# Hybrid decoder trunk on one core: the mixer's tables, taps and first output units in another order, and three smaller rearrangements

## The chip, the core and the metric

The kernel runs on one core of one Trainium2 chip. The metric is the device time of one execution in microseconds (us), the median of several runs. A core has TensorE (PE in the rows; PEld is its weight load), VectorE (DVE), ScalarE (ACT), GpSimd (POOL) and SyncE (SP), which here only issues transfers.

## The reference, cut to what matters

One sequence of 256 tokens with 16 learned positions in front (272 positions, width 1024) goes through two layers and a last RMSNorm, all in float32.

```python
for layer in range(2):
    if layer == 0:
        h = h + even_mixer(rms_norm(h, g), ...)     # recurrent block (RG-LRU) and a state space model (S5), side by side
        h = h + swiglu(rms_norm(h, g), w_gate, w_up, w_down)          # dense, 3072 wide
    else:
        h = h + gla_mixer(rms_norm(h, g), ...)                        # chunked gated linear attention
        h = h + moe_swiglu(rms_norm(h, g), router_w, ...)             # top 2 of 8 experts, each 3584 wide
return rms_norm(h, final_norm)[:, 16:]

def even_mixer(h, ...):
    z = h @ w_in                                    # 1024 gate columns, 1024 recurrent columns, 512 S5 columns
    rec = rg_lru(causal_conv(recurrent), ...)       # a = exp(-8 r softplus(-lam)); b = sqrt(1 - a^2) * i * x; h = a h + b
    a_out = gelu(gate) * rec
    b_out = s5_ssm(s5_columns, ...)                 # complex diagonal states, 32 groups of 16 channels, then a GLU
    return concatenate([a_out, b_out]) @ w_out
```

## The kernel before

Positions lie along the free dimension (272 columns), channels on the 128 partitions, eight chunks of 128 channels. Stages follow each other: mixer (to about 178 us), dense SwiGLU (to about 400), attention (to about 555), experts (to about 1549), last norm.

**Weights.** All weights come as tiles of 1 MB (class `Stream`, DMA line L115 on SyncE's queue, tile number = place in the file). Two units of 1024 columns make a tile. Some matrices are used as float32 as they are (`fraw`, L245). For the others (`fs`, `out_part`, lines L224 to L226) a unit is first split into two parts: `split` lets ScalarE copy the high part (`whi`, L144) and VectorE subtract it for the low part (`wlo`, L146), and each product takes three matmuls. `st.unit(u)` splits unit u and the two behind it. Until the attention stage the tiles lie in a ring of R1 = 3 buffers (`ring1`), so a load can start when a buffer's last reader is through. The mixer's input units are tiles 0 to 11 (two column blocks of S5 input, then `rec`, `gates` and `zgate` blocks in the order of MIX_ORDER: tile 9 holds zgate 2 and 3, tile 10 zgate 4 and 5, tile 11 zgate 6 and 7), tile 12 the GLU, tile 13 and on the output projection, whose first unit is `B_OUT // 8`.

**Order.** PE, ACT, DVE and POOL run their instructions in the order in which the code is written (`manual_schedule`). `step(o, evac, n)` runs what is due, lets `evac` be run one step later, and runs n entries of the list `fill`. In the mixer `fill` holds the S5 tables (`tables`, L527 to L529, twelve pieces that grow from 16 to 512 columns, all on DVE) and the S5 state pieces. The SP queue is sorted by the framework.

**Mixer around the change.** `rec(m)` makes one block of the recurrent branch; its evacuation is one ACT instruction (L575) and three of DVE (L578) into `xc`. `gates(b)` multiplies blocks 2b and 2b+1 of `xc`. `s5_tp` and `s5_x` (L591, L602) prepare the S5 input. `zgate(m)` makes one block of the gate branch, evacuated by ACT (L562). There are four PSUM buffers for these blocks (tag "mm"). `lru_exp` is 16 ACT instructions (L690, L691), `lru_sqrt` four (L695), `lru_scan(b)` four of DVE (L698 to L701). `s5_direct(cc)` (L654) makes the S5 taps of one quarter in PSUM (`kp`); `s5_taps` copies them (ACT L659, POOL L660) and `s5_shift` places them with ten transfers into `KT` (L668). `out_taps(3)` is some 9 us of POOL. Then `s5_local` (L798, reads KT), `s5_out` (L810), `mix_lru` (DVE L839, then high part `mh` on ACT L829 and low part `ml` on POOL L831), and the output projection `out_part` (tiles wo).

```python
        zgate(2, 3)
        s5_x(7)
        fill.extend(s5_states(1))
        for b in range(4):
            lru_exp(b)
        s5_direct(0)
        zgate(3, 2)
```

**Dense stage.** `resid_add` adds the mixer's output, and `split_chunk` writes the eight chunks of `xg` (ACT L258, DVE L259), one by one. Group m = 0 of the dense stage needs all eight in turn, first for gate, then for up. `norm_mm` (L280) sums the squares; its result is first needed by the evacuation of gate 0.

**Start and end.** At the start SP issues the first four loads of `hT` and the two halves of tile 0. At the end the last expert's second half (`yps`) is split into `Y` high and low (L1496, L1497), `combine` multiplies both by a one-hot matrix (L1501, L1502) and adds into X (L1504), then `squares`, `gains` (L1562) and `finish` (L1565 on, output DMA L1571).

Of the kernel before, what the change touches and what calls it, by code (L numbers as in the profile page):

```python
# [8 lines left out]
F32 = mybir.dt.float32  # L9
# [7 lines left out]
P = 128  # L17
# [151 lines left out]
def trunk(ctx: ExitStack, tc: tile.TileContext, xt, pv, pw, cst, gfin, wf, wm, out, dbg=None):  # L169
# [25 lines left out]
    pwt = resid.tile([P, NPW - 1024], F32, name="pwt")  # L195
    nc.sync.dma_start(pvt, pv)
    st.load_to(0)
    nc.sync.dma_start(hT[:, 0:2], xsrc[:, 0:2])
    nc.sync.dma_start(st.raw[0][:, :UW], wf[0, :, :UW])
    for a in range(2, ND, 2):  # L200
        nc.sync.dma_start(hT[:, a:a + 2], xsrc[:, a:a + 2])
    nc.sync.dma_start(st.raw[0][:, UW:], wf[0, :, UW:])
# [109 lines left out]
    with ExitStack() as mx:  # L312
# [255 lines left out]
        def rec(m, n=0):  # L568
            b, j = divmod(m, 2)
            if j == 0:  # L570
                xc[b] = slot(f"xc{b}")
            x_ = xc[b][:, j]

            def evac(o):
                act.activation(x_, o, AF.Identity, scale=cw[:, 3, m:m + 1], bias=pvs("conv_b")[:, m:m + 1])  # L575
                for k in range(3):
                    d = 3 - k
                    dve.scalar_tensor_tensor(x_[:, d:], o[:, :NT - d], cw[:, k, m:m + 1], x_[:, d:], op0=ALU.mult,  # L578
                                             op1=ALU.add)

            step(fraw(B_REC[m], 8, raw_x(xn), NT), evac, n)
# [136 lines left out]
        shuffle()  # L718
        rec(1, 1)
        rec(2, 1)  # L720
        rec(3, 3)
        halves(C0[0][:, :, None], lambda o, sl: act.activation(o[:, :, 0], cre[sl], AF.Copy))
        halves(C0[1][:, :, None], lambda o, sl: act.activation(o[:, :, 0], cim[sl], AF.Copy, scale=-1.0))
        powers()
        gates(0)
        bg(2)
        rec(4, 2)
        s5_tp(0)
        rec(5, 2)
# [29 lines left out]
        out_taps(1)  # L759
        gated(3)  # L760
        out_taps(2)
        zgate(2, 3)
        s5_x(7)
        fill.extend(s5_states(1))
        for b in range(4):
            lru_exp(b)
        s5_direct(0)
        zgate(3, 2)
        for b in range(4):
            lru_sqrt(b)  # L770
        s5_direct(1)
        lru_scan(0)
        zgate(4, 2)
        s5_direct(2)
        lru_scan(1)
        zgate(5, 2)
        s5_direct(3)
        s5_taps()
        s5_shift()
        out_taps(3)  # L780
        lru_scan(2)
        zgate(6, 20)
# [62 lines left out]
        s5_local(1)  # L845
        s5_out(0)
        low = mix_lru(2, low)
        st.unit(B_OUT // 8)
        s5_out(1)
        low = mix_lru(3, low)  # L850
        low()
# [50 lines left out]
    with ExitStack() as fx:  # L902
        fp = phase(fx, "fp")
        fw = phase(fx, "fw", 4)
        ph = fp.tile([P, NFF, NT], F32R, name="ph")
        pl = fp.tile([P, NFF, NT], F32R, name="pl")
        zgs = {}

        def gate_evac(m, o):
            zg = zgs[m] = fw.tile([P, NT], F32, name="zg")  # L910
            dve.tensor_tensor(zg, o, rstd, op=ALU.mult)
            if m:
                after(1, lambda: act.activation(zg, zg, AF.Silu))
            else:
                act.activation(zg, zg, AF.Silu)

        def up_evac(m, o):
            zg = zgs.pop(m)
            zu = fw.tile([P, NT], F32, name="zu")
            dve.tensor_tensor(zu, o, rstd, op=ALU.mult)  # L920
            dve.tensor_tensor(zu, zu, zg, op=ALU.mult)
            after(1, lambda: act.activation(ph[:, m], zu, AF.Copy))
            after(2, lambda: dve.tensor_tensor(pl[:, m], zu, ph[:, m].bitcast(F32), op=ALU.subtract))

        for m in range(NFF):
            lag = 3 if m == 0 else 1
            if m == 1:
                norm_mm()
            step(fs(B_F + 16 * m, 8, xs_norm(), NT), lambda o, m=m: gate_evac(m, o), lag=lag)
            step(fs(B_F + 16 * m + 8, 8, xs_norm(), NT), lambda o, m=m: up_evac(m, o), lag=lag)  # L930
# [567 lines left out]

    def combine(e, d, i):
        o = psum("x", "cmb")  # L1500
        pe.matmul(o, OHT[e][:, i], Ys[e, d][0], start=True, stop=False)  # L1501
        pe.matmul(o, OHT[e][:, i], Ys[e, d][1], start=False, stop=True)  # L1502
        a = X[:, i, 512 * d:512 * d + 512]
        dve.scalar_tensor_tensor(a, o, gat[:, i, e:e + 1], a, op0=ALU.mult, op1=ALU.add)  # L1504

    hcur = None
    for s in range(E * NF + 1):
# [42 lines left out]
    fs4 = ep.tile([P, 2, 2], F32, name="fs4")  # L1550
    fs2 = ep.tile([P, 2], F32, name="fs2")

    def part(t, i, d):
        return t[:, i, 512 * d:512 * d + 512]

    def squares(d):
        for i in range(2):
            act.activation(sqs[:, i], part(X, i, d), AF.Square, accum_out=fs4[:, i, d:d + 1])

    def gains(d):  # L1560
        for i, eng in enumerate((dve, pool)):
            eng.tensor_tensor(part(ys, i, d), part(X, i, d), gft[:, 512 * d:512 * d + 512], op=ALU.mult)  # L1562

    def finish():
        dve.tensor_tensor(fs2, fs4[:, :, 0], fs4[:, :, 1], op=ALU.add)  # L1565
        inv_root(fs2, fs2, D)
        for d in range(2):
            act.activation(part(ys, 1, d), part(ys, 1, d), AF.Copy, scale=fs2[:, 1:2])
            dve.tensor_scalar(part(ys, 0, d), part(ys, 0, d), fs2[:, 0:1], None, op0=ALU.mult)
            for i in range(2):  # L1570
                nc.sync.dma_start(out[P * i:P * i + P, 512 * d:512 * d + 512], part(ys, i, d))  # L1571

    sqs = ew.tile([P, 4, 512], F32, name="sqs", tag="xq0", bufs=1)
    ys = ew.tile([P, 2, D], F32, name="ys", tag="xq1", bufs=1)
# [11 lines left out]
    with tc.If(cnt > CAP):  # L1586
# [200 lines left out]
```

## Time and profile before

| what | value |
|---|---|
| runs shown | 1566.23, 1572.45, 1572.51 us; median 1572.45 |
| profiled execution, its own time | 1565.07 us |
| its span | 1563.0 us |
| TensorE busy | 1521.8 us (97%) |
| VectorE busy | 1297.5 us (83%) |
| ScalarE busy | 1055.9 us (68%) |

The time of the profiled execution is 2.1 us above its span. Times in the rows count from the start of the span. A busy TensorE is no TensorE at its peak: matmuls overlap and their ends are modelled, so what is read is where its instructions start and what the idle time before one waited for.

### The profile page before, as it was taken

The page shows a single profiled execution, that of the slowest core. Times are in us where ns is not written, and L with a number is a line of the kernel's source. Part 1 is how long each engine was busy: PE and PEld are TensorE (multiplying, and loading weights), DVE is VectorE, ACT ScalarE, POOL GpSimd, SP SyncE. Part 2 cuts the span into 40 slices and gives each one's busy share as a digit, 9 for nine tenths or more (in the row PEclk, how much of TensorE's full clock was granted, in tenths as well). Part 3 has the DMA queues.
Part 4 walks back from the last instruction along what each step waited for, and adds up shares of the span by engine and source line. Part 5 has one row for each costly group of instructions (what it writes and reads, how often), then busy time and mean ns, then how long its engine had stood idle before and what let it go on. Part 6 is the DMA issues. An engine that isn't in the chain of part 4 may idle for free.

```text
span 1563.0 us, 21942 instructions
## 1 busy us (share of the span) xinstructions
PE 1521.8 (97%) x8306; PEld 1317.7 (84%) x8306; DVE 1297.5 (83%) x1464; ACT 1055.9 (68%) x1297; POOL 165.4 (11%) x260
## 2 busy tenths in 40 slices
PE   8998999999989989999999999999999999999996
PEld 7788999999889977888888888888888888888885
DVE  5687676655595669999999999999999999999996
ACT  3345544444543578887887787887887887777875
POOL 8952100001251200000000000000000000000000
PEclk9999999999999999999999999999999999999998
DMA  7333455454336758999899999999999999999960
GB/s 249 116 119 117 165 183 186 163 184 168 111 105 243 275 204 311 366 376 354 335 365 356 373 366 352 347 365 352 365 367 365 362 351 353 360 365 373 356 240 30
DMA packets 68897, 433.56 MB, mean 277 GB/s; under 512 B 14384, under 2 KB 14768, under 8 KB 17072
## 3 DMA queue, kind: packets, MB, share of 16 engines
q1 hardware_dynamic: 68784, 432.09, 74.2%
q8 instruction: 67, 1.10, 0.3%
q14 instruction: 46, 0.38, 0.1%
HBM read 429.80 MB, written 1.05 MB: 276 GB/s over the span
## 4 chain that ended last, share of the span: by engine, by line
PE 82%; DVE 4%; issue 3%; ACT 2%; POOL 0%; DVEq 0%; ACTq 0%; POOLq 0%
PE gu L1455 13%; PE gu L1457 13%; PE gu L1456 13%; PE yp L1484 7%; PE yp L1486 7%; PE yp L1485 7%; PE acc L225 5%; PE acc L224 5%; PE acc L226 5%; PE etp L1465 2%; DVE wlo L146 1%; ACT whi L144 1%; PE cmb L1502 0%; PE cmb L1501 0%; PE go L225 0%
## 5 line engine op out<-in xcount | busy, mean ns | idle before, releaser
L146 DVE TENSOR_TENSOR wlo<-raw,whi 128x1024 fp32r<-128x1024 f32 x788 | 959.3, 1236 | 130.7 <-ACT whi L144 99.1
L144 ACT ACTIVATE whi<-raw 128x1024 fp32r<-128x1024 f32 x788 | 825.0, 1060 | 261.6 <-PE acc L225 99.3
L1455 PE MATMUL gu<-whi,xq 128*128 128x512 f32 x896 | 357.7, 399 | 0.7 <-ACT whi L144 0.7
L1456 PE MATMUL gu<-wlo,xq 128*128 128x512 f32 x896 | 350.3, 391 | 2.4 <-DVE wlo L146 2.4
L1457 PE MATMUL gu<-whi,xq 128*128 128x512 f32 x896 | 351.5, 392 | 0.0
L1456 PEld LDWEIGHTS gu<-wlo,xq 128*128 128x128 f32 x896 | 168.5, 188 | 38.4 <-DVE wlo L146 4.2
L1457 PEld LDWEIGHTS gu<-whi,xq 128*128 128x128 f32 x896 | 168.3, 188 | 37.9
L1455 PEld LDWEIGHTS gu<-whi,xq 128*128 128x128 f32 x896 | 168.5, 188 | 34.8 <-ACT whi L144 1.5
L1484 PE MATMUL yp<-whi,hh 128*128 128x512 f32 x448 | 176.0, 393 | 0.0
L1486 PE MATMUL yp<-whi,hlw 128*128 128x512 f32 x448 | 175.7, 392 | 0.0
L1485 PE MATMUL yp<-wlo,hh 128*128 128x512 f32 x448 | 174.9, 390 | 0.0
L224 PE MATMUL acc<-xg,whi 128*128 128x272 f32 (+1 forms) x576 | 169.6, 294 | 1.7 <-DVE slab L1116 0.9
L226 PE MATMUL acc<-xg,wlo 128*128 128x272 f32 (+1 forms) x576 | 167.3, 290 | 1.9 <-DVE wlo L146 1.9
L225 PE MATMUL acc<-xg,whi 128*128 128x272 f32 (+1 forms) x576 | 166.9, 290 | 0.8 <-DVE xg L259 0.5
L224 PEld LDWEIGHTS acc<-xg,whi 128*128 128x128 f32 x576 | 110.1, 191 | 3.4 <-DVE slab L1116 1.3
L226 PEld LDWEIGHTS acc<-xg,wlo 128*128 128x128 f32 x576 | 109.8, 191 | 2.2 <-DVE wlo L146 2.2
L225 PEld LDWEIGHTS acc<-xg,whi 128*128 128x128 f32 x576 | 110.1, 191 | 1.5 <-DVE xg L259 1.4
L1562 POOL TENSOR_TENSOR ys<-X,gft 128x512 f32<-128x512 f32 x2 | 2.9, 1456 | 996.0 <-DVE X L1504 996.0
L1486 PEld LDWEIGHTS yp<-whi,hlw 128*128 128x128 f32 x448 | 84.2, 188 | 18.9
L1485 PEld LDWEIGHTS yp<-wlo,hh 128*128 128x128 f32 x448 | 84.2, 188 | 18.7 <-DVE wlo L146 0.3
L1484 PEld LDWEIGHTS yp<-whi,hh 128*128 128x128 f32 x448 | 84.2, 188 | 17.5
L245 PE MATMUL acc<-xfn,raw 128*128 128x272 f32 x320 | 77.6, 400 | 5.7 <-DMA raw<-in_wf_dram 5.7
(522 smaller groups left out, 1753.5 us busy)
## 6 DMA issues: line engine op xcount, KB each, us to landing
raw<-in_wm_dram SPq DMA_DIRECT2D x334, 1024.0 KB, 6.4
raw<-in_wf_dram SPq DMA_DIRECT2D x70, 1024.0 KB, 4.9
raw<-in_wm_dram SPq DMA_DIRECT2D x4, 512.0 KB, 6.8
hT<-in_xt_dram SPq DMA_DIRECT2D x4, 272.0 KB, 4.4
raw<-in_wf_dram SPq DMA_DIRECT2D x2, 512.0 KB, 5.3
out_dram<-ys SPq DMA_DIRECT2D x4, 256.0 KB, 3.4
KT<-k SPq DMA_DIRECT2D x10, 64.0 KB, 2.3
U<-uA SPq DMA_DIRECT2D x16, 34.0 KB, 2.1
```

Of the source, the lines that this page charges most:

```text
L144: nc.scalar.activation(hi, w, AF.Copy)
L146: nc.vector.tensor_tensor(lo, w, hi.bitcast(F32), op=ALU.subtract)
L224: pe.matmul(o, wh, xh, start=start, stop=False)
L225: pe.matmul(o, wh, xl, start=False, stop=False)
L226: pe.matmul(o, wl, xh, start=False, stop=stop)
L245: pe.matmul(o, w[:, c:c + P], xs(k), start=(k == 0), stop=(k == nblk_k - 1))
L1455: pe.matmul(o, XG[e][:, 0, k], hi[:, c], start=(k == 0), stop=False)
L1456: pe.matmul(o, XG[e][:, 0, k], lo[:, c], start=False, stop=False)
L1457: pe.matmul(o, XG[e][:, 1, k], hi[:, c], start=False, stop=(k == ND - 1))
L1484: pe.matmul(o, hh[:, j], hi[:, c], start=(f == 0 and j == 0), stop=False)
L1485: pe.matmul(o, hh[:, j], lo[:, c], start=False, stop=False)
L1486: pe.matmul(o, hlw[:, j], hi[:, c], start=False, stop=(f == NF - 1 and j == 3))
```

## The change

Mixer: the table pieces are given out later and in fours (`rec(4, 4)`, `rec(5, 4)`), so that three of them no longer stand ahead of the evacuation of `rec(3)`; `s5_direct`, `s5_taps` and `s5_shift` move up by one or two zgate blocks; and `st.unit(B_OUT // 8)`, which splits the first three units of the output projection (both halves of tile 13, the first of tile 14), moves from behind `s5_out(0)` to ahead of `lru_exp`. Dense stage: gate 0 and up 0 are run in turns, chunks 0 to 5 of both, then 6 and 7 of both. Start: tile 0's first half is loaded in two pieces from ScalarE's queue. End: the last half is multiplied by one float32 matmul instead of two, the product with the norm's gain of the first half moves up, that of the second half is joined with the scaling, and the four output transfers go to two queues.

```diff
     st.load_to(0)
+    nc.scalar.dma_start(st.raw[0][:, :2 * P], wf[0, :, :2 * P])
     nc.sync.dma_start(hT[:, 0:2], xsrc[:, 0:2])
-    nc.sync.dma_start(st.raw[0][:, :UW], wf[0, :, :UW])
+    nc.scalar.dma_start(st.raw[0][:, 2 * P:UW], wf[0, :, 2 * P:UW])
...
-        rec(3, 3)
+        rec(3)
...
         gates(0)
-        bg(2)
-        rec(4, 2)
+        rec(4, 4)
         s5_tp(0)
-        rec(5, 2)
+        rec(5, 4)
         s5_tp(1)
         gates(1)
...
         out_taps(2)
+        s5_direct(0)
         zgate(2, 3)
         s5_x(7)
         fill.extend(s5_states(1))
+        out0 = st.unit(B_OUT // 8)
         for b in range(4):
             lru_exp(b)
-        s5_direct(0)
+        s5_direct(1)
         zgate(3, 2)
         for b in range(4):
             lru_sqrt(b)
-        s5_direct(1)
+        s5_direct(2)
+        s5_direct(3)
         lru_scan(0)
         zgate(4, 2)
-        s5_direct(2)
+        s5_taps()
+        s5_shift()
         lru_scan(1)
         zgate(5, 2)
-        s5_direct(3)
-        s5_taps()
-        s5_shift()
         out_taps(3)
...
         low = mix_lru(2, low)
-        st.unit(B_OUT // 8)
         s5_out(1)
...
+        first = [(st.unit(B_F // 8 + w), psum("mm", "acc")) for w in range(2)]
+        for k0, k1 in ((0, 6), (6, 8)):
+            for w in range(2):
+                (hi, lo), o = first[w]
+                for k in range(k0, k1):
+                    c = k * P
+                    mm3(o[:, :NT], hi[:, c:c + P], lo[:, c:c + P], *xs_norm()(k), k == 0, k == 7)
+        after(2, lambda: gate_evac(0, first[0][1][:, :NT]))
+        after(2, lambda: up_evac(0, first[1][1][:, :NT]))
...
+        if len(Ys[e, d]) == 2:
...
+        else:
+            pe.matmul(o, OHT[e][:, i].bitcast(F32), Ys[e, d][0], start=True, stop=True)
...
-            unload(E - 1, 1)
+            gains(0)
+            Ys[E - 1, 1] = [ew.tile([P, 512], F32, name="Yf", tag="xq2", bufs=1)]
+            act.activation(Ys[E - 1, 1][0], yps[E - 1, 1], AF.Copy)
...
-    gains(0)
     squares(1)
-    gains(1)
     finish()
```

ScalarE's queue from zgate 1's evacuation on (gz0 is zgates 0 and 1, gz1 zgates 2 and 3; raw_856 is tile 13, raw_858 tile 14), before:

```order
L562 ACTIVATE gz0_707<-acc_742 128x272
L603 ACTIVATE X11_352<-xp_838 128x272 [waits PE_49]
L690 ACT_TABLE_LOAD
L690 ACTIVATE av0_844<-ra0_463,spl_105 128x272 [waits Pool_49]
L691 ACTIVATE ra0_463<-ra0_463,spl_105 128x272 [waits Activation_49]
```

and with the change:

```order
L563 ACTIVATE gz0_708<-acc_743 128x272
L604 ACTIVATE X11_353<-xp_848 128x272 [waits PE_49]
L144 ACTIVATE whi_862<-raw_856 128x1024 [waits DMAHW2_49]
L144 ACTIVATE whi_866<-raw_856 128x1024
L144 ACTIVATE whi_872<-raw_858 128x1024 [waits DMAHW3_49]
L691 ACT_TABLE_LOAD
L691 ACTIVATE av0_876<-ra0_455,spl_106 128x272 [waits Pool_49]
```

Three splits with waits for transfers now stand ahead of the sixteen instructions of `lru_exp` and of zgate 2's evacuation, which follows them.

SyncE's queue around the ten KT transfers, before (raw_909 is tile 12, raw_990 tile 13):

```order
L115 DMA raw_909<-in_wf_dram 128x2048 [waits DMAHW5_49,DMAHW0_49,PE_49]
L115 DMA raw_990<-in_wf_dram 128x2048 [waits DMAHW6_49,PE_49]
L668 DMA KT_188<-k0_962 32x16x32 [waits Activation_49,Pool_49]
L668 DMA KT_188<-k0_962 32x16x32 x2
L668 DMA KT_188<-k0_962 32x16x32 [waits Pool_49]
```

and with the change (raw_854 is tile 12, raw_860 tile 15):

```order
L115 DMA raw_854<-in_wf_dram 128x2048 [waits DMAHW6_49,DMAHW1_49,PE_49]
L115 DMA raw_856<-in_wf_dram 128x2048 [waits DMAHW7_49,PE_49]
L115 DMA raw_858<-in_wf_dram 128x2048 [waits DMAHW2_49,DVE_49]
L669 DMA KT_189<-k0_965 32x16x32 [waits Activation_49,Pool_49]
L669 DMA KT_189<-k0_965 32x16x32 x2
L669 DMA KT_189<-k0_965 32x16x32 [waits Pool_49]
L669 DMA KT_189<-k0_965 32x16x32 [waits DMAHW0_49]
L115 DMA raw_860<-in_wf_dram 128x2048 [waits DMAHW1_49,PE_49]
L669 DMA KT_189<-k0_965 32x16x32
```

Tile 14's load now stands ahead of the KT transfers and waits for VectorE where it waited for TensorE, and tile 15's load stands among them. In the built program tile 13 waits in both kernels for the last matmul of zgate 5; tile 14 now waits for the low part of tile 13's second half; tile 15 waits for the last matmul of zgate 7.

VectorE's queue around the evacuation of `rec(3)` (three instructions into the second half of xc1; acc is the block's PSUM buffer, Ec and Es the tables) before:

```order
L578 SCALAR_TENSOR_TENSOR xc1_399<-acc_400,pvt_71,xc1_399 128x271 [waits DVE_49]
L527 TENSOR_TENSOR ta__323<-Ec_310 128x16 [waits Pool_49]
L528 TENSOR_TENSOR tb__324<-Es_311 128x16 [waits Pool_49]
L529 TENSOR_TENSOR Ec_310<-ta__323,tb__324 128x16 [waits DVE_49]
L527 TENSOR_TENSOR ta__323<-Ec_310,Es_311 128x16 [waits DVE_49]
```

and with the change:

```order
L579 SCALAR_TENSOR_TENSOR xc1_400<-acc_401,pvt_71,xc1_400 128x271 [waits DVE_49]
L579 SCALAR_TENSOR_TENSOR xc1_400<-acc_420,pvt_71,xc1_400 128x269 [waits Activation_49]
L579 SCALAR_TENSOR_TENSOR xc1_400<-acc_420,pvt_71,xc1_400 128x270 [waits DVE_49]
L579 SCALAR_TENSOR_TENSOR xc1_400<-acc_420,pvt_71,xc1_400 128x271 [waits DVE_49]
L528 TENSOR_TENSOR ta__324<-Ec_311 128x16 [waits Pool_49]
```

The second block of xc1 is now written ahead of the first table piece, which waits for POOL.

## Rows read from the trace of the kernel before

**Rows 1.** The page: head, chain that ended last by engine, one costly group.
```profile
span 1563.0 us, 21942 instructions
...
PE 82%; DVE 4%; issue 3%; ACT 2%; POOL 0%; DVEq 0%; ACTq 0%; POOLq 0%
...
L146 DVE TENSOR_TENSOR wlo<-raw,whi 128x1024 fp32r<-128x1024 f32 x788 | 959.3, 1236 | 130.7 <-ACT whi L144 99.1
```

**Rows 2.** Timeline of TensorE, mixer: start, us, what, [idle before <- releaser].
```profile
49.64 0.62 PE L245 MATMUL acc<-xc,raw 128*128 128x272 f32 x2
...
54.42 2.07 PE L245 MATMUL acc<-xc,raw 128*128 128x272 f32 x8 [1.25 <-DVE xc L578]
...
86.86 3.88 PE L245 MATMUL acc<-xfn,raw 128*128 128x272 f32 x16
...
102.38 1.87 PE L654 MATMUL kp<-C,BP 128*128 128x32 f32 x16
104.08 3.91 PE L245 MATMUL acc<-xfn,raw 128*128 128x272 f32 x16
...
119.09 3.76 PE L798 MATMUL yp<-U,KT 128*128 128x68 f32 x32 [1.97 <-issue]
...
132.28 0.59 PE L226 MATMUL wo<-mh,wlo 128*128 128x272 f32 x1 [0.95 <-DVE wlo L146]
```

**Rows 3.** Timeline of ScalarE, 92 to 133 us.
```profile
92.04 1.28 ACT L690 ACT_TABLE_LOAD   x1
...
101.09 0.38 ACT L562 ACTIVATE gz<-acc 128x272 f32<-128x272 f32 x1
...
129.70 2.94 ACT L144 ACTIVATE whi<-raw 128x1024 fp32r<-128x1024 f32 x3
```

**Rows 4.** Timeline of VectorE, 49 to 129 us.
```profile
49.85 1.56 DVE L578 SCALAR_TENSOR_TENSOR xc<-acc,pvt,xc 128x269 f32<-128x269 f32 x3
...
103.46 0.73 DVE L698 SCALAR_TENSOR_TENSOR ra<-av,ra 128x544 f32<-128x544 f32 x1 [4.84 <-ACT ra L695]
...
126.67 1.97 DVE L839 TENSOR_TENSOR ix<-ix,gz 128x544 f32<-128x544 f32 x3
```

**Rows 5.** Load of tile 13: issue (ns), start us, time to landing.
```profile
L115 SPq DMA_DIRECT2D raw<-in_wf_dram x1: 327/327/327, 108.0 to 108.0; - x1
...
DMA to landing us min/median/max: 4.8/4.8/4.8
```

**Rows 6.** Timeline of SyncE's queue: the ten transfers into KT.
```profile
110.41 6.65 SPq L668 DMA_DIRECT2D KT<-k  x10
```

**Rows 7.** Windows: us; busy PE, PEld, DVE, ACT, POOL; granted clock; DMA share; GB/s.
```profile
133.00:134.00 1.00, 1.00 (x6) 1.00 (x5) 1.00 (x1) 0.22 (x1) 0.43 (x1) 0.50 0.00 0
...
135.00:136.00 1.00, 1.00 (x8) 1.00 (x8) 1.00 (x2) 0.00 (x0) 0.00 (x0) 0.77 0.53 74
```

**Rows 8.** Timeline of GpSimd: low parts of the mixer's result.
```profile
128.19 5.24 POOL L831 TENSOR_TENSOR ml<-ix,mh 128x544 fp32r<-128x544 f32 x3 [6.73 <-issue]
```

**Rows 9.** Timeline of all engines at the start.
```profile
1.64 0.43 SPq L199 DMA_DIRECT2D raw<-in_wf_dram  x1
```

**Rows 10.** Timeline of TensorE: first dense groups, the norm's sum, matmuls behind.
```profile
178.13 0.29 PE L224 MATMUL acc<-xg,whi 128*128 128x272 f32 x1
...
187.75 0.62 PE L280 MATMUL ssq<-sqacc,ones 128*128 128x272 f32 x2
...
191.10 0.29 PE L226 MATMUL acc<-xg,wlo 128*128 128x272 f32 x1
...
194.89 0.29 PE L226 MATMUL acc<-xg,wlo 128*128 128x272 f32 x1
```

**Rows 11.** Timeline of all engines at the end.
```profile
1552.16 2.35 DVE L1562 TENSOR_TENSOR ys<-X,gft 128x512 f32<-128x512 f32 x2
...
1552.87 0.19 ACT L1558 ACTIVATION_READ_ACCUMULATOR sqs<-X 128x1 f32 x1
...
1555.65 1.91 SPq L1571 DMA_DIRECT2D out_dram<-ys  x4
```

More of the change, by code (lines that the diff above doesn't have):

```diff
@@ L734, in trunk @@
         s5_tp(2)
-        rec(6, 1)
+        rec(6, 2)
         s5_x(1)
         s5_tp(3)
-        rec(7, 1)
+        rec(7, 2)
         s5_x(2)
@@ L923, in up_evac @@
             after(2, lambda: dve.tensor_tensor(pl[:, m], zu, ph[:, m].bitcast(F32), op=ALU.subtract))
-        for m in range(NFF):
-            lag = 3 if m == 0 else 1
+        first = [(st.unit(B_F // 8 + w), psum("mm", "acc")) for w in range(2)]
[7 more added lines that the diff above has]
+        after(2, lambda: up_evac(0, first[1][1][:, :NT]))
+        for m in range(1, NFF):
             if m == 1:
                 norm_mm()
-            step(fs(B_F + 16 * m, 8, xs_norm(), NT), lambda o, m=m: gate_evac(m, o), lag=lag)
-            step(fs(B_F + 16 * m + 8, 8, xs_norm(), NT), lambda o, m=m: up_evac(m, o), lag=lag)
+            step(fs(B_F + 16 * m, 8, xs_norm(), NT), lambda o, m=m: gate_evac(m, o))
+            step(fs(B_F + 16 * m + 8, 8, xs_norm(), NT), lambda o, m=m: up_evac(m, o))
         def ffn_add(m, o):
@@ L1500, in combine, with part, squares, gains @@
         o = psum("x", "cmb")
-        pe.matmul(o, OHT[e][:, i], Ys[e, d][0], start=True, stop=False)
-        pe.matmul(o, OHT[e][:, i], Ys[e, d][1], start=False, stop=True)
+        if len(Ys[e, d]) == 2:
+            pe.matmul(o, OHT[e][:, i], Ys[e, d][0], start=True, stop=False)
+            pe.matmul(o, OHT[e][:, i], Ys[e, d][1], start=False, stop=True)
+        else:
+            pe.matmul(o, OHT[e][:, i].bitcast(F32), Ys[e, d][0], start=True, stop=True)
         a = X[:, i, 512 * d:512 * d + 512]
         dve.scalar_tensor_tensor(a, o, gat[:, i, e:e + 1], a, op0=ALU.mult, op1=ALU.add)
+    fs4 = ep.tile([P, 2, 2], F32, name="fs4")
+    fs2 = ep.tile([P, 2], F32, name="fs2")
+    ysl = []
+    def part(t, i, d):
+        return t[:, i, 512 * d:512 * d + 512]
+    def squares(d):
+        sqs = ew.tile([P, 2, 512], F32, name="sqs", tag="xq0", bufs=1)
+        for i in range(2):
+            act.activation(sqs[:, i], part(X, i, d), AF.Square, accum_out=fs4[:, i, d:d + 1])
+    def gains(d):
+        if not d:
+            ysl[:] = [ew.tile([P, 2, D], F32, name="ys", tag="xq1", bufs=1)]
+        for i, eng in enumerate((dve, pool)):
+            eng.tensor_tensor(part(ysl[0], i, d), part(X, i, d), gft[:, 512 * d:512 * d + 512], op=ALU.mult)
+    def finish():
+        ys = ysl[0]
+        dve.tensor_tensor(fs2, fs4[:, :, 0], fs4[:, :, 1], op=ALU.add)
+        inv_root(fs2, fs2, D)
+        for i in range(2):
+            act.activation(part(ys, i, 0), part(ys, i, 0), AF.Copy, scale=fs2[:, i:i + 1])
+            dve.scalar_tensor_tensor(part(ys, i, 1), part(X, i, 1), fs2[:, i:i + 1], gft[:, 512:], op0=ALU.mult,
+                                     op1=ALU.mult)
+            for d, eng in enumerate((nc.scalar, nc.sync)):
+                eng.dma_start(out[P * i:P * i + P, 512 * d:512 * d + 512], part(ys, i, d))
     hcur = None
@@ L1547, in trunk @@
                     unload(e - 1, d)
[L1550 to L1574, printed above, removed]
     squares(0)
@@ L1642, in trunk @@
                     dve.scalar_tensor_tensor(a, o, gat[:, i, e:e + 1], a, op0=ALU.mult, op1=ALU.add)
-        sqs = ew.tile([P, 4, 512], F32, name="sqs", tag="xq0", bufs=1)
-        ys = ew.tile([P, 2, D], F32, name="ys", tag="xq1", bufs=1)
+        gains(0)
         for d in range(2):
             squares(d)
-            gains(d)
         finish()
```

## The prediction, made before the result was known

> **What bounds the kernel now.** The page first: the chain that ended last is 82% TensorE [rows 1], so what counts is where TensorE waits, and the rest of the working stays with the stages that the diff touches: start, mixer, first dense groups, end. The profiled execution took 1565.07 us. The median of the runs, 1572.45, lies 7.4 above it, so the sum is made against 1565.07 and 7.4 is put on top at the end.
>
> In the mixer's TensorE timeline [rows 2] three waits are to be seen. Gates(1), sixteen matmuls, runs from 49.64 to 56.49 (54.42 + 2.07), 6.85 us where such a block takes 3.88; it waits for `xc` from VectorE, which writes it at 49.85 [rows 4]. Before `s5_local` at 119.09 stands an idle time of 1.97, and before the third matmul of the output projection (132.28) one of 0.95 for its low part. In ScalarE's timeline [rows 3] the table load of `lru_exp` starts at 92.04 and zgate 2's evacuation at 101.09, and VectorE's first `lru_scan` follows at 103.46 after 4.84 us of waiting for ScalarE [rows 4]. So between 92 and 104 us ScalarE is the critical engine of the recurrent branch. In SyncE's queue tile 13 is issued at 108.0 and takes 4.8 us to land [rows 5], and the ten transfers into KT go out from 110.41, 0.665 us apart [rows 6].
>
> **The change part by part. Tables.** The evacuation of rec(3) goes ahead of the table pieces, so gates(1) runs at 3.88 instead of 6.85: −3.0 us for TensorE. The pieces go later, where VectorE waits for ScalarE anyway; if they don't find room the end of the chain is no earlier, and the price is 0 to 3.0.
>
> **Early split.** This decides the case. Three splits of tiles 13 and 14 now stand on ScalarE's queue ahead of `lru_exp`'s sixteen activations and zgate 2's evacuation. Tile 13's load waits for zgate 5's last matmul, in both kernels, because it takes zgate 4 and 5's buffer. Before, nobody minded: it was issued at 108.0 and split at 129.70 [rows 3]. Now `lru_exp`, which before began at 92.04, waits for it. Step by step, in the clock of the trace:
>
> Zgate 5 is 3.0 earlier by the tables and 1.7 later by one more kp block ahead of it (102.38 to 104.08 [rows 2]): tile 13 is issued at 108.0 − 3.0 + 1.7 = 106.7 and lands at 111.5. Two high parts at 0.98 (2.94 / 3 [rows 3]): 113.5. The low part of the second at 1.24 [rows 1]: 114.7. Only then may tile 14's load start, since the built order makes it wait for that low part: issued 114.9, landed 119.7, high part done 120.7. From the table load to zgate 2's evacuation takes 101.09 − 92.04 = 9.05, so the latter starts at 129.75 instead of 101.09. `lru_scan` follows 2.37 later (103.46 − 101.09), at 132.1: VectorE's chain is 28.7 late.
>
> TensorE is held by the same. There are four PSUM buffers, so zgates 2 to 5 go ahead, and zgate 6 waits for zgate 2's evacuation, to about 130.3. It has then stood idle for some 24 us. What such a pause does to its clock is read from the output projection: after two waits the granted clock was 0.50 from 133 to 134 us and 0.77 from 135 to 136 [rows 7], that is about 3.3 us at 1.2 GHz instead of 2.4, which costs 1.6. Zgates 6 and 7 are two blocks of sixteen matmuls, 2 × 3.8 undisturbed (one is modelled at 3.91 [rows 2]), so they end at 130.3 + 7.6 + 1.6 = 139.5. Zgate 7 also releases tile 15's load, and this one now stands in the middle of the KT transfers on SyncE's queue: five behind it, 3.3 us at 0.665 [rows 6], to 143.0. The last of the ten was issued before at 110.41 + 6.65 = 117.06, 2.0 ahead of `s5_local` [rows 2]: `s5_local` starts at 145.0 instead of 119.09. From there to the first two matmuls of the output projection it was 11.7 before the 0.95 wait (132.28 − 0.95 − 119.09, with some 0.8 of another wait in it), so about 11 now, and 1.6 more if the clock is low again: 156 to 158.
>
> VectorE's way to the same place: its first product with the gate starts at 126.67 + 28.7 = 155.4, takes 0.66 (1.97 / 3 [rows 4]), then ScalarE's high part, about the same, and GpSimd's low part 1.75 (5.24 / 3 [rows 8]): 158.4. Both ways meet near 158, and the splits are long done. Against 132.28 this is +26.1. The low clock that the projection paid there (1.6) is not paid again, as TensorE will have run since 145; the next chunk's low part on GpSimd gives back 0.5 of it. **Mixer: +25**, the −3.0 of the tables, the vanished waits for KT and for the splits all inside. Bounds: +22, if both low clocks are spared and the chain runs shorter as its neighbours are idle; +31, if the low clock holds through zgates 6 and 7 (see the third rival).
>
> A rule speaks to this. In the trace zgate 2's matmuls end at 90.7 (86.86 + 3.88 [rows 2]) and their evacuation, which nothing else holds, runs at 101.09 behind the sixteen activations [rows 3]: ScalarE did not pull it forward. The Trainium skill, "Perfetto Trace Analysis", section "Tensor Engine Instruction (MATMUL, LD_WEIGHTS)", says that the queues of ScalarE and VectorE are strict FIFO, while TensorE's has a limited reorder. By that rule the waiting split stops all behind it, +25; if ScalarE could run past it, the sum would be that of the first rival.
>
> **Start.** One issue of 0.43 [rows 9] leaves SyncE's queue for ScalarE's: −0.3, from −1.2 (if the smaller first piece lands earlier) to +0.4 (if the `hT` loads collide with it).
>
> **Dense.** The first two groups run from 178.13 to the norm's sum at 187.75, 9.6 us, since each chunk of `xg` comes late [rows 10]. Thirty matmuls behind take 194.89 − 191.10 = 3.79, 0.126 each; 48 are 6.1. In turns, the first six chunks serve two groups while the last two are made: up to −3.5. Gate 2 may then wait some 0.5 for gate 0's evacuation, which needs the norm: **−3.1**, from −2.0 to −3.5.
>
> **End.** VectorE's two products with the gain, 1552.16 to 1554.51, stand ahead of the sum of the squares, whose last part is ready at 1553.06 [rows 11]. One goes earlier and one into the scaling: −1.4. Four output transfers at 0.48 (1.91 / 4) on two queues instead of one save about one issue, −0.5, and the scaling with two operands costs +0.2: **−1.7**, from −0.8 to −2.5. The single float32 matmul in place of two halves spares the low part of Y, and its size is open; I take 0.
>
> The Trainium skill, "Trainium Kernel Development and Optimization", Quick Reference, Key Constraints, says that transfers from SyncE's, ScalarE's and GpSimd's queues run on the same 16 engines and that several queues save the issue time alone. By it the start gains at most 0.43 and the end the one issue; no run here shows it yet.
>
> **Sum:** 25 − 0.3 − 3.1 − 1.7 = +19.9, so 1585.0 by the profiled execution and 1592 by the median.
>
> **The rivals.** First, and on the other side: **the splits don't hold ScalarE**, because tiles 13 and 14 are in the ring when it comes to them. That needs both loads issued by about 82 us, which only a free buffer gives. Then the splits cost ScalarE 2.94 us, which the tables' 3.0 just cover; the mixer gains the waits at the projection, some 2.3, and the whole is −2.3 − 0.3 − 3.1 − 1.7 = −7.4, about 1565. The point from which it decides is the issue of tile 13: each microsecond after 87 costs one. For it speaks that three buffers are many for units that TensorE takes 8 us each; against it that the load of tile 13 was seen at 108.0 and that the order leaves its wait as it was. It is also the case in which the change does what it looks like. Second, **only tile 13 holds**: if tile 14 is issued together with it, the 6.2 us from 113.5 to 119.7 go, and the time is 1586. Against it stands the wait for VectorE in the built order. Third, **the clock stays low** through zgates 6 and 7 after 24 us of idleness: they take 7.6 more instead of 1.6, KT and `s5_local` come 6 later, 1598. For it: no wait of the mixer in the trace is as long; against it: the granted clock came back within about 3.3 us in [rows 7].
>
> **How the numbers follow.** Forecast 64%, third rival 18%, second 10%, first 8%. The mixer's bounds with the other terms as taken (22 − 5.1 and 31 − 5.1, that is +17 and +26) give 1589 to 1598; the second rival and a run as fast as the lowest of before (6 under the median) take the lower end to 1580, the third with the upper bounds of start and end the upper one to 1601. Faster or slower means by more than 0.5% (7.9 us), about what a measurement of this kernel tells from no change. The first rival at 1565 lies at that limit: half of it is faster (0.04), half the same (0.04); all others are slower, 0.92.
>
> **What would show it.** In the changed kernel's profile ScalarE should be idle from about 88 to 111 us, ahead of a split, released by a DMA; tile 13 issued near 107 and tile 14 near 115; zgate 2's evacuation near 130; TensorE idle from about 107 to 130 and running zgate 6 at 1.2 GHz for the first microseconds; `s5_local` near 145; gates(1) without a wait; first dense groups in about 6.5 us. I am wrong if tile 13 is issued before 90 us, if zgate 6 starts before 115, or if TensorE finds other work in that hole.

## The result: slower by 1.8%, and where the time went

| kernel | median us | runs | ratio to the runs of before, 95% interval |
|---|---|---|---|
| before | 1572.48 | 1566.23 to 1574.65 (6) | |
| changed | 1600.07 | 1597.98 to 1601.32 (6) | 1.0179 [1.0159, 1.0199] |

The changed kernel is 27.6 us slower by the medians. The two profiled executions lie further apart, 1565.07 and 1601.32 us (spans 1563.0 and 1599.2), since the executions of the kernel before fall into two groups, some 1566 and some 1573 us, and its first profile is of the lower one; experiments 6 and 7 show why.

The page of the changed kernel: its head, the busy tenths of TensorE and its granted clock in forty slices of 40 us, and the chain that ended last.

```profile
span 1599.2 us, 21934 instructions
...
PE   8974999999998989999999999999999999999997
...
PEclk9986799999999999999999999999999999999999
...
PE 91%; DVE 3%; issue 2%; ACT 2%; DMA 1%; POOL 0%; SPq 0%; ACTq 0%; DVEq 0%; POOLq 0%
```

The damage sits in the third to fifth slice (80 to 200 us): TensorE is busy 0.7 and 0.4 there and its clock reads 0.8, 0.6 and 0.7. ScalarE's timeline (start us, us, what, [idle before <- releaser]) shows the cause; it is to be read beside [rows 3].

```profile
92.31 0.40 ACT L604 ACTIVATE X<-xp 128x272 f32<-128x272 f32 x1 [5.66 <-PE xp L603]
115.34 2.00 ACT L144 ACTIVATE whi<-raw 128x1024 fp32r<-128x1024 f32 x2 [22.64 <-DMA raw<-in_wf_dram]
123.60 1.06 ACT L144 ACTIVATE whi<-raw 128x1024 fp32r<-128x1024 f32 x1 [6.26 <-DMA raw<-in_wf_dram]
124.68 1.28 ACT L691 ACT_TABLE_LOAD   x1
...
133.72 0.38 ACT L563 ACTIVATE gz<-acc 128x272 f32<-128x272 f32 x1
```

ScalarE waits 22.64 us for tile 13, then 6.26 for tile 14. The table load of `lru_exp` starts at 124.68 where it started at 92.04, and zgate 2's evacuation is at 133.72 instead of 101.09. TensorE's timeline is to be read beside [rows 2].

```profile
51.55 3.83 PE L246 MATMUL acc<-xc,raw 128*128 128x272 f32 x16
...
97.61 3.73 PE L655 MATMUL kp<-C,BP 128*128 128x32 f32 x32
101.16 9.21 PE L246 MATMUL acc<-xfn,raw 128*128 128x272 f32 x32
134.15 9.78 PE L246 MATMUL acc<-xfn,raw 128*128 128x272 f32 x32 [23.79 <-ACT gz L563]
151.83 7.07 PE L799 MATMUL yp<-U,KT 128*128 128x68 f32 x32 [7.90 <-DMA KT<-k]
158.69 13.65 PE L811 MATMUL yp<-S,CP 128*128 128x68 f32 x63
...
172.31 0.57 PE L225 MATMUL wo<-mh,whi 128*128 128x272 f32 x1
```

Gates(1) at 51.55 takes 3.83 us without a wait (before 6.85): the tables do what they should. Then TensorE idles 23.79 us for zgate 2's evacuation and 7.90 for KT. Behind the second hole `s5_local` and `s5_out` take 20.5 us (151.83 to 172.31); in [rows 2] both began at 119.09, and `s5_out` was through by 130. `s5_out` and a window (columns as in [rows 7]) in the kernel before:

```profile
122.68 7.31 PE L810 MATMUL yp<-S,CP 128*128 128x68 f32 x64
```

```profile
122.00:124.00 2.00, 2.00 (x20) 2.00 (x20) 2.00 (x5) 0.00 (x0) 0.00 (x0) 1.00 0.03 8
```

The windows of the changed kernel (us; busy time and count of PE, PEld, DVE, ACT, POOL; granted clock; DMA share; GB/s) say why.

```profile
102.00:104.00 2.00, 2.00 (x5) 1.44 (x5) 0.00 (x0) 0.00 (x0) 0.00 (x0) 0.50 0.00 0
...
132.00:134.00 2.00, 0.00 (x0) 0.00 (x0) 0.00 (x0) 1.94 (x5) 0.00 (x0) 0.50 0.00 0
...
140.00:144.00 4.00, 3.93 (x18) 2.92 (x16) 4.00 (x4) 0.43 (x2) 3.92 (x5) 1.00 0.50 77
...
148.00:150.00 2.00, 0.00 (x0) 0.00 (x0) 2.00 (x2) 0.00 (x0) 1.87 (x3) 0.71 1.02 191
...
168.00:172.00 4.00, 4.00 (x21) 4.00 (x20) 0.00 (x0) 0.40 (x1) 0.11 (x1) 0.50 0.00 0
...
176.00:180.00 4.00, 4.00 (x33) 4.00 (x32) 3.83 (x12) 3.10 (x6) 0.00 (x0) 0.98 0.78 260
```

The clock falls in each hole (0.50 by 132, 0.71 at 148 to 150). Behind the first it is back at 1.00 by 140; behind the second it stays at 0.50, that is 1.2 GHz, through all of `s5_local` and `s5_out`, in which TensorE is busy without a gap, and comes back only in the output projection. The first row shows one more fall, at 101 us, with TensorE busy and without a wait, right behind the two kp blocks at 97.61; zgates 4 and 5 take 9.21 us there, and 7.58 in experiment 3, where the clock did not fall. SyncE's queue, to be read beside [rows 6]:

```profile
138.55 3.29 SPq L669 DMA_DIRECT2D KT<-k  x5
143.96 0.33 SPq L115 DMA_DIRECT2D raw<-in_wf_dram  x1
144.34 4.98 SPq L669 DMA_DIRECT2D KT<-k  x5
```

Tile 15's load stands in the middle of the KT transfers, as the order showed, and waits for zgate 7; the five behind it take 4.98 us instead of 3.3, beside a load of 1 MB.

The stages of the diff behind the mixer, TensorE first (beside [rows 10]), then the end (beside [rows 11]):

```profile
217.67 0.28 PE L225 MATMUL acc<-xg,whi 128*128 128x272 f32 x1
...
223.72 0.62 PE L281 MATMUL ssq<-sqacc,ones 128*128 128x272 f32 x2
```

```profile
1590.05 0.19 ACT L1529 ACTIVATION_READ_ACCUMULATOR sqs<-X 128x1 f32 x1
1590.27 0.16 DVE L1539 TENSOR_TENSOR fs<-fs 128x2 f32<-128x2 f32 x1 [0.79 <-ACT sqs L1529]
...
1591.75 0.39 ACTq L1546 DMA_DIRECT2D out_dram<-ys  x1
```

The first dense groups start 39.5 us later than before (217.67 against 178.13) and take 6.05 us instead of 9.62: −3.6. The end, from the last matmul of the last product (1548.5 before, 1585.6 now) to the span's end, is 13.6 us instead of 14.5: −0.9. The sum over the squares' parts no longer waits for the products with the gain, but from the first output transfer to the end it is 7.45 us as it was 7.35, so the second queue gains nothing. Sum by the traces: 39.5 − 3.6 − 0.9, and 1.2 that the two traces differ in between, 36.2. In the 39.5 are 1.9 us by which this profile is late before any wait, at gates(1) (51.55 against 49.64).

### The profile page after: what moved, and what is told of

Read it like the earlier page. It is cut to its first block, busy times and chain, and to the rows that moved or that the text cites. A ratio compares the mean times of both kernels' runs of the same rounds, so it can differ in the third digit from the quotient of the medians.

```text
span 1599.2 us, 21934 instructions
## 1 busy us (share of the span) xinstructions
PE 1534.2 (96%) x8306; PEld 1329.6 (83%) x8306; DVE 1291.7 (81%) x1462; ACT 1057.1 (66%) x1297; POOL 164.8 (10%) x259
## 4 chain that ended last, share of the span: by engine, by line
PE 91%; DVE 3%; issue 2%; ACT 2%; DMA 1%; POOL 0%; SPq 0%; ACTq 0%; DVEq 0%; POOLq 0%
PE gu L1464 13%; PE gu L1466 13%; PE gu L1465 12%; PE yp L1493 6%; PE yp L1495 6%; PE acc L246 6%; PE yp L1494 6%; PE acc L226 5%; PE acc L225 5%; PE acc L227 5%; PE etp L1474 2%; PE yp L811 1%; DVE wlo L146 1%; PE wo L225 1%; PE wo L227 1%
## 5 line engine op out<-in xcount | busy, mean ns | idle before, releaser
L1493 PE MATMUL yp<-whi,hh 128*128 128x512 f32 x448 | 176.1, 393 | 0.0
L246 PE MATMUL acc<-xfn,raw 128*128 128x272 f32 x320 | 82.5, 419 | 30.2 <-ACT gz L563 23.8
L246 PEld LDWEIGHTS acc<-xfn,raw 128*128 128x128 f32 x320 | 64.6, 205 | 44.6 <-ACT gz L563 24.2
```

What stands on the lines that cost most here:

```text
L246: pe.matmul(o, w[:, c:c + P], xs(k), start=(k == 0), stop=(k == nblk_k - 1))
L1493: pe.matmul(o, hh[:, j], hi[:, c], start=(f == 0 and j == 0), stop=False)
```

## The experiments

The common indentation of every diff is cut. Times are medians; ratios are to the runs of the kernel before that ran beside them.

**1. Only the early split put back.**

```diff
-out0 = st.unit(B_OUT // 8)
 for b in range(4):
     lru_exp(b)
...
 low = mix_lru(2, low)
+st.unit(B_OUT // 8)
 s5_out(1)
```

> The changed kernel with only the early split of the output projection's first units put back behind s5_out(0), its old place; all else of the change stays. Theory (the early split alone makes the loss, because ScalarE's queue stops at it): gates(1) keeps its 3.0 us, the dense turns their 3.6 and the end its 0.9 of gain, the start keeps its 1.9 of loss, so about 5.6 us under the kernel before, 1567, and no wait of ScalarE near 92 us. Rival (the new places of the taps, the KT transfers or the loads at the start make a good part of the loss): above the kernel before, 1578 to 1595.

1561.21 us (1559.74 to 1562.90, 9 runs), ratio 0.9939 [0.9921, 0.9957]. The one line is worth 38.9 us, and without it the change is a gain. Against before that is 8.8 by the medians and 3.4 by the profiled executions (1565.07 and 1561.69), as this kernel has one group of times only. It is some 6 under the expected 1567, which was reckoned from a median of the upper group. Its TensorE no longer waits ahead of `s5_local`, where [rows 2] had 1.97 us, since KT is placed earlier:

```profile
116.97 3.68 PE L798 MATMUL yp<-U,KT 128*128 128x68 f32 x32
```

By experiments 6 and 7 this wait is where the upper group of before comes from, so some 4 of the 8.8 (1569.98 less the lower group's 1566) are probably the earlier KT; no run has that part of the change alone. Against the profile of before, the mixer itself gains nothing: VectorE's chain and the third matmul of the projection stand where they stood in [rows 4] and [rows 2] (103.46 and 132.28). VectorE, then TensorE:

```profile
103.58 0.73 DVE L699 SCALAR_TENSOR_TENSOR ra<-av,ra 128x544 f32<-128x544 f32 x1 [6.82 <-ACT ra L696]
```

```profile
132.50 0.60 PE L227 MATMUL wo<-mh,wlo 128*128 128x272 f32 x1 [0.76 <-DVE wlo L146]
```

The 3.0 us of the tables were, by these profiles, spent on the kp block that now stands ahead of zgate 2 (1.75), and on a first norm's sum that came at 12.53 instead of 11.18 us.

**2. Only the early split, in the kernel before.**

```diff
 fill.extend(s5_states(1))
+st.unit(B_OUT // 8)
 for b in range(4):
     lru_exp(b)
...
 low = mix_lru(2, low)
-st.unit(B_OUT // 8)
 s5_out(1)
```

> The kernel before with only the early split moved ahead of lru_exp. Theory: the loss of the whole change without its gains of some 5.6 us, so 33 us over the kernel before, about 1606. Rival (the split is harmless unless the taps and the KT transfers stand where the change puts them): under 1590.

1601.10 us, ratio 1.0204 [1.0168, 1.0240], against 1569.98 for before: +31, or +35 against the lower group of before. The split alone makes the whole loss; 1606 was some 5 too high: it was reckoned as if the rest of the change gained in the mixer here too, but the projection of this kernel starts at 169.18, 3.1 us ahead of the changed kernel, whose clock had fallen at 101 us already.

**3. Only the splits of tile 13 early.** `st.unit` runs there with a depth of two, the third split stands in its old place.

```diff
-out0 = st.unit(B_OUT // 8)
+st.depth = 2
+st.unit(B_OUT // 8)
+st.depth = 3
...
 low = mix_lru(2, low)
+st.unit(B_OUT // 8)
 s5_out(1)
```

> The changed kernel with only the two splits of tile 13 early; the third, of tile 14, stands where it stood in the kernel before. Theory (ScalarE's queue waits once for each load): ScalarE goes on at 117.4 instead of 124.7, all behind it 7.3 us earlier, 1593. Rival (what ends last is tile 15's load, the KT transfers behind it and TensorE's low clock, not the second wait): 1598 to 1601.

1591.69 us, ratio 1.0137 [1.0105, 1.0168], 8.4 under the changed kernel. ScalarE goes on right behind the first two splits:

```profile
112.55 2.00 ACT L144 ACTIVATE whi<-raw 128x1024 fp32r<-128x1024 f32 x2 [20.79 <-DMA raw<-in_wf_dram]
...
123.61 0.38 ACT L563 ACTIVATE gz<-acc 128x272 f32<-128x272 f32 x1
```

So the queue does wait once for each load, and the second wait was priced about right (1593 was expected); zgate 2's evacuation comes 10.1 us earlier than in the changed kernel, 2.8 of them because tile 13 was there earlier.

**4. TensorE kept busy in the holes.** Matmuls into a PSUM tile that nobody reads, ahead of zgate 6 and of `s5_local`; the stall of ScalarE stays.

```diff
+dum = []
...
+def idle(t, n):
+    if not t:
+        t.append(psum("x", "dum"))
+    o = t[0][:, :NT]
+    for i in range(n):
+        pe.matmul(o, raw_x(xn)(0)[:, :P], raw_x(xn)(i % 8), start=True, stop=True)
...
+idle(dum, n1)
 zgate(6, 20)
...
+idle(dum, n2)
 s5_local(0)
```

| n1, n2 | median us | ratio | zgate 6 starts | s5_local to projection |
|---|---|---|---|---|
| 0, 0 (changed kernel) | 1600.07 | 1.0179 | 134.15 | 151.83 to 172.31 |
| 98, 24 | 1608.78 | 1.0250 [1.0214, 1.0287] | 154.49 | 172.82 to 183.5 |
| 98, 0 | 1598.64 | 1.0189 [1.0153, 1.0226] | 151.97 | 159.31 to 169.9 |
| 46, 11 | 1595.78 | 1.0172 [1.0140, 1.0205] | 131.18 | 147.37 to 167.8 |
| 46, 0 | 1599.95 | 1.0184 [1.0151, 1.0218] | 135.22 | 151.44 to 171.9 |
| 46, 20 | 1588.65 | 1.0119 [1.0084, 1.0155] | 131.30 | 149.59 to 160.2 |

> The changed kernel with TensorE kept busy where it stands idle: 98 matmuls into an unused PSUM tile ahead of zgate 6 and 24 ahead of s5_local; nothing reads them. The ten KT transfers also stand ahead of tile 15's load here. Theory (idle time of TensorE lets its clock fall, and the work behind the idle time pays for it): granted clock 1.0 from 112 us on, zgates 6 and 7 in 7.6 us instead of 9.8, s5_local and s5_out in 10.9 instead of 20.5; VectorE's and GpSimd's way then ends last, near 162.7 instead of 172.3, so about 9.5 us under the changed kernel, 1590. Rival (the low clock has nothing to do with idleness, or the stall of ScalarE is all of the loss): 1598 to 1601.

> As the kernel with both fillers, but with the 98 matmuls ahead of zgate 6 alone. Theory: zgates 6 and 7 run at the full clock, KT lands near 147.5 and no longer behind tile 15; TensorE then idles some 5.5 us ahead of s5_local, its clock falls there, and s5_local and s5_out take up to 20 us again, so 4 us under the changed kernel, 1596. Rival (only the first, long idle time of 24 us costs clock): as with both fillers, 1590.

Both first sizes were wrong: a filling matmul took 0.457 us, not half of it, so 98 of them outlasted the hole by some 20 us. The second kernel, with 98 and none, is the plainest of all. Its zgate 6 starts 17.8 us later than in the changed kernel, and its time is nearly the same: the wait of 7.90 us ahead of `s5_local` is gone as well, and without a hole TensorE does the rest of the mixer at the full clock.

```profile
151.97 7.50 PE L246 MATMUL acc<-xfn,raw 128*128 128x272 f32 x32
159.31 3.68 PE L809 MATMUL yp<-U,KT 128*128 128x68 f32 x32
162.83 7.31 PE L821 MATMUL yp<-S,CP 128*128 128x68 f32 x64
```

> As the first kernel with fillers, with their sizes mended: in the first one each filling float32 matmul took 0.457 us, twice what was reckoned, so the fillers outlasted the holes. Now 46 of them (21 us) ahead of zgate 6 and 11 (5.0 us) ahead of s5_local. Theory (the low clock behind the holes costs some 10 us of the loss): zgates 6 and 7 and s5_local with s5_out at the full clock, the output projection starts near 162.7 instead of 172.3, held by VectorE's and GpSimd's way, 1590. Rival (the stall of ScalarE is all): 1598 to 1601.

> As the kernel with both mended fillers, without the second: TensorE is idle for some 6 us ahead of s5_local and no longer for 24 ahead of zgate 6. Theory (a hole of 6 us is enough for the clock to fall): s5_local and s5_out at 1.2 GHz for most of their length, 1595. Rival (only the long hole costs clock): 1590 as with both.

Neither time was met: with 46 and 11 the time was 1596, not 1590, and without the second filler 1600, not 1595. In the second the clock had also fallen at 100 us (zgates 4 and 5 took 10.44 us), so not all of its 4 us more are the missing filler's. In the first a hole of 3.32 us was left ahead of `s5_local`, and the clock fell in it. Its rows, TensorE and two windows:

```profile
147.37 7.07 PE L809 MATMUL yp<-U,KT 128*128 128x68 f32 x32 [3.32 <-DMA KT<-k]
154.23 13.86 PE L821 MATMUL yp<-S,CP 128*128 128x68 f32 x64
```

```profile
144.00:146.00 2.00, 0.05 (x1) 0.00 (x0) 2.00 (x3) 0.00 (x0) 1.85 (x3) 1.00 1.11 147
...
154.00:160.00 6.00, 6.00 (x31) 6.00 (x30) 5.86 (x8) 1.57 (x3) 2.03 (x2) 0.50 0.01 3
```

So the long hole is not where the clock costs most: zgates 6 and 7 took 7.82 us behind the first filler and 9.78 without it, 2.0 us. The short one ahead of `s5_local` is.

> As the kernel with 46 and 11 filling matmuls, with 20 in the second place (9.1 us), so that they last until KT has landed; there a hole of 3.3 us was left ahead of s5_local, and s5_local and s5_out ran at 1.2 GHz. Theory (this short hole alone costs some 10 us): no wait ahead of s5_local, granted clock 1.0 through s5_out, about 11 us for both instead of 20.7, the output projection near 160 to 164 instead of 168 to 172, about 1588 to 1590. Rival (the clock falls behind the stall anyway): 1595 to 1600 as before.

1588.65 us: closing this hole is worth 7.1 us against the kernel that left it (1595.78), and 11.4 against the changed kernel, with ScalarE's stall still there. TensorE's rows:

```profile
131.30 9.29 PE L246 MATMUL acc<-xfn,raw 128*128 128x272 f32 x32 [2.75 <-ACT gz L563]
...
149.59 3.68 PE L809 MATMUL yp<-U,KT 128*128 128x68 f32 x32
153.11 7.31 PE L821 MATMUL yp<-S,CP 128*128 128x68 f32 x64
```

The projection starts at 160.2, held by ScalarE's high parts (157.32) and GpSimd's low parts, as VectorE's chain lets it. In these kernels the KT transfers stand a little otherwise in SyncE's queue than in the changed kernel (three or all ten of them ahead of tile 15's load, not five), and zgate 6 starts 2.9 us earlier here; both are part of the 11.4, but not of the 7.1, as the kernel with 46 and 11 has three ahead too and starts zgate 6 at 131.18. Zgates 6 and 7 take 9.29 us: the clock fell behind the 2.75 us that the first filler left, though not behind the 2.60 us with 46 and 11.

**5. The loads at the start put back as well.**

```diff
-nc.scalar.dma_start(st.raw[0][:, :2 * P], wf[0, :, :2 * P])
 nc.sync.dma_start(hT[:, 0:2], xsrc[:, 0:2])
-nc.scalar.dma_start(st.raw[0][:, 2 * P:UW], wf[0, :, 2 * P:UW])
+nc.sync.dma_start(st.raw[0][:, :UW], wf[0, :, :UW])
```

> The changed kernel with the early split and the loads at the start put back, all else as changed. Against the kernel with only the split put back (1561.2): theory (the new loads at the start cost up to 1.9 us, as the first norm's sum came at 13.09 instead of 11.18): 1559 to 1560. Rival (the start makes no difference): 1561.

1561.45 us (1559.87 to 1563.32, 10 runs) against 1561.21: no difference. The first norm's sum comes between 11.2 and 13.2 us with either order of the loads in the profiles of this study, so the 1.9 us that the first two profiles showed there were chance.

**6. Four filling matmuls in the kernel before**, ahead of `s5_local`, where it waits 1.97 us [rows 2].

```diff
+dum = psum("x", "dum")[:, :NT]
+for i in range(4):
+    pe.matmul(dum, raw_x(xn)(0)[:, :P], raw_x(xn)(i), start=True, stop=True)
 s5_local(0)
 s5_local(1)
```

> The kernel before with four filling matmuls (1.8 us) in the wait of 1.97 us ahead of s5_local. The times of the kernel before lie in two groups, 1565 to 1569 at a mean granted clock of 0.990 and 1571 to 1575 at 0.983 to 0.987. Theory (in the second group the clock falls in this wait, as it does behind the longer waits of the changed kernel): all runs between 1564 and 1569 at 0.990. Rival (the groups come from elsewhere): two groups as before, median 1569 to 1573.

1565.69 us (1564.13 to 1569.13, 12 runs, mean granted clock 0.990 to 0.993), ratio 0.9972 [0.9955, 0.9989]. Beside it 21 runs of the kernel before: 8 between 1565.38 and 1567.20 at 0.990, 13 between 1571.60 and 1574.82 at 0.982 to 0.986. The upper group is gone. Of all 50 runs of the kernel before that are compared here, 18 lie below 1568.3, 28 above 1571 and 4 between, so the groups are not quite apart.

**7. The kernel before, profiled again.**

> The kernel before, unchanged, to have a second profile of it. Theory: if its time is of the upper group (1571 to 1575), the granted clock is 0.50 in s5_local and s5_out (119 to 130 us in the first profile, there 1.00), and both take 8 to 10 us longer; if it is of the lower group, the profile is as the first. Rival: a time of the upper group with the full clock there.

It took 1572.26 us, so it is of the upper group. TensorE and two windows:

```profile
121.28 6.62 PE L798 MATMUL yp<-U,KT 128*128 128x68 f32 x32 [1.96 <-issue]
127.69 13.86 PE L810 MATMUL yp<-S,CP 128*128 128x68 f32 x64
```

```profile
120.00:122.00 2.00, 0.72 (x6) 0.75 (x6) 1.91 (x2) 1.99 (x3) 1.85 (x3) 0.94 0.90 160
122.00:124.00 2.00, 2.00 (x11) 2.00 (x11) 1.95 (x2) 1.36 (x3) 1.60 (x2) 0.50 0.94 393
```

The same wait, 1.96 us, and behind it the clock is at 0.50 and the two stages take 20 us instead of 11. The two profiles are 7.5 us apart in all; `s5_local` starts 2.2 us later in this one already, as it was late ahead of the wait (121.28 against 119.09), so not all of this pair's difference is the clock.

**8. What is left of the change, with the split where its data has landed.** As experiment 5, the first kp block behind zgate 2 again, and the three high parts made by ScalarE behind the gelu of the gates, the low parts by VectorE where they were.

```diff
...
-s5_direct(0)
 zgate(2, 3)
...
-out0 = st.unit(B_OUT // 8)
...
+s5_direct(0)
 s5_direct(1)
 zgate(3, 2)
...
 for c in range(4):
     act.activation(gz[c], gz[c], AF.Gelu_apprx_tanh)
+for v in range(3):
+    st.high(B_OUT // 8 + v)
...
 low = mix_lru(2, low)
+st.unit(B_OUT // 8)
 s5_out(1)
```

> The change without what hurts it: loads at the start as before, the first quarter of the taps behind zgate 2 again, and the early split put where its data has landed: the three high parts on ScalarE behind the four gelu of the gates, the low parts on VectorE where they were. Theory: in the kernel with only the split put back (1561) VectorE's chain began at 103.58, no earlier than before, since 1.4 us at the start and 1.75 us of the kp block ahead of zgate 2 ate the 3.0 of the tables; without them it begins near 100.4, and the projection's waits for its first split (2 us) go: 1556 to 1557. Rival (the chain is held elsewhere): 1559 to 1562.

1559.40 us (1558.55 to 1560.58, 6 runs), ratio 0.9933 [0.9910, 0.9957]: the fastest here, though some 3 above what was expected and within the rival's 1559 to 1562 (a chain held elsewhere), and its interval overlaps that of experiment 1. VectorE's chain starts at 101.33 (expected 100.4), and the projection earlier than in experiment 1, at 127.14 instead of 131.05. Its timeline shows what takes it back:

```profile
127.14 0.37 PE L233 MATMUL wo<-mh,whi 128*128 128x272 f32 x1
127.89 0.39 PE L234 MATMUL wo<-ml,whi 128*128 128x272 f32 x1 [0.38 <-POOL ml L839]
128.98 0.39 PE L235 MATMUL wo<-mh,wlo 128*128 128x272 f32 x1 [0.69 <-DVE wlo L155]
...
130.19 0.39 PE L234 MATMUL wo<-ml,whi 128*128 128x272 f32 x1 [0.31 <-POOL ml L839]
```

It now waits for GpSimd's low parts and VectorE's `wlo`, and the first dense groups start only 2.2 earlier than in experiment 1 (176.1 against 178.3).

## Why the prediction held, and where it did not

The mechanism was the one named: three splits on ScalarE's queue, waits for tile 13 and tile 14, zgate 2's evacuation and VectorE's chain behind them. Experiments 1 to 3 show it apart from the rest. The waits in ScalarE's timeline were foreseen at the right places, and nothing passed the waiting split of 22.64 us: zgate 2's matmuls end at 91.43, and their evacuation runs at 133.72. The rows agree with the rule of strict FIFO that was weighed there (the Trainium skill, "Perfetto Trace Analysis", section "Tensor Engine Instruction (MATMUL, LD_WEIGHTS)").

| step | predicted | measured |
|---|---|---|
| tile 13 issued, landed | 106.7, 111.5 | 110.4, 115.3 |
| tile 14 issued, third split done | 114.9, 120.7 | 118.8, 124.7 |
| zgate 2 evacuated, first `lru_scan` | 129.8, 132.1 | 133.7, 136.1 |
| zgate 6 starts; 6 and 7 take | 130.3; 9.2 | 134.2; 9.8 |
| last KT transfer issued | 143.0 | 149.3 |
| `s5_local` starts | 145.0 | 151.8 |
| from there to the projection | 11 to 13 | 20.5 |
| mixer | +25 | +39.5, of it 1.9 late from the start on |
| start | −0.3 | none that can be measured (experiment 5) |
| dense | −3.1 | −3.6 |
| end | −1.7 | −0.9 |
| sum, from trace to trace | +19.9 | +36.2 |

**The term that failed is the mixer's, by 14.5 us, and within it the low clock.** "1.6 more if the clock is low again" was taken for `s5_local` and `s5_out`, from the 3.3 us that the clock needed to come back in the output projection [rows 7]. Behind the hole it didn't come back for 20 us, which cost some 9 us. The third rival had such a case and its time, 1598, but in the wrong place: behind the long hole, at zgates 6 and 7, where the clock cost 2.0. What else was short: the loads, late by 3.8 us. Of these 1.9 were there from the start of this profile on, and some 1.6 came from the fall of the clock at 101 us, for some 3.4 us with TensorE busy (first row of the windows above); without this fall (experiment 3) ScalarE had tile 13 at 112.55, a microsecond from the forecast. And the transfers into KT shared the engines with tile 15, 4.98 us for five instead of 3.3.

**The step from the trace to the median failed too,** the other way. The 7.4 us were put on top as if they went with any kernel. Experiments 6 and 7 show that they are the low clock in `s5_local` and `s5_out`, which the kernel before has in more than half of its runs; in the changed kernel it is in the profile already, and its runs agree with the profile within 3.3 us. So 1592 came near 1600 by two errors that partly cancel: 14.5 + 1.8 too little, 7.4 too much, which is luck. The range held it by its upper end, which stood on the third rival's low clock in the wrong place.

**The tables** gave their 3.0 us where it was said, and in experiment 1 the mixer still ended no earlier: the prediction put the moved kp block only ahead of zgate 5 and not on ScalarE's way, though it stands ahead of zgate 2 and of the product of `s5_x(7)`, which ScalarE evacuates right ahead of `lru_exp`. Experiment 8, which moves it back, starts VectorE's chain at 101.33, 1.6 us ahead of experiment 5 (102.89). **The end** was over-sized by the second output queue, and the start by its loads. Neither gained what can be measured, though one issue takes 0.43 us at the start [rows 9] and 0.48 at the end [rows 11]. The rule that several queues save the issue time alone (the Trainium skill, "Trainium Kernel Development and Optimization", Quick Reference, Key Constraints) would have allowed no more than these, and the runs show not even that. What the single float32 matmul does there was not tried apart, and the 1.2 us between the dense stage and the end, in which the code is the same, were not followed up.

Open is why the clock fell at about 101 us in the changed kernel, with no gap in TensorE's work. The change itself puts two kp blocks one behind the other. In the ten profiles of kernels with such a pair the clock fell in one or right behind it in six (the changed kernel, experiments 1, 5 and 8, and the fillers of 98 and 24 and of 46 and 0); in the four profiles of kernels in which the kp blocks stand apart (before, twice, and experiments 2 and 6) it fell at none. That the pair is the cause is not shown, as no run parts the blocks alone.

## What to carry to other kernels

A split or a copy that is moved up takes its wait along, and on an in-order queue the wait is everybody's: before moving it, look up when its load can be issued, which is when its buffer comes free, and put it no earlier than where that load has landed. Price a hole in TensorE's work by what runs behind it, at either clock, and not only by its length. And where a kernel's runs fall into two groups, find out which of them the profile shows before carrying a difference from trace to median.

## What the runs showed of the hardware

The granted clock fell to half (0.50, that is 1.2 GHz) in or right behind waits of TensorE of 3.32 and 2.75 us (experiment 4), but stayed at 1.00 behind waits of 2.60 and 2.81 us there. Behind one of 1.96 and 1.97 us in the kernel before it fell in one profile and not in the other, with the same program. Without any wait it fell in or behind two kp blocks run one after the other in six profiles of ten.

It came back 2.3 to 4.7 us into the output projection in the profiles in which `s5_local` and `s5_out` ran at 0.50, but not during the 20 us of gapless work in these two. In the kernel before a wait of 2 us cost some 7 us more than itself (1573 against 1566), and four matmuls whose result nobody reads took that away in all of 12 runs.
